# A two-layer decoder trunk on one core: the feed-forward's weight high part streams the tokens' high and low parts as one 512-column matmul

## The chip, the cores and the metric

One core of a Trainium2 chip runs the whole program in one launch. The metric is the device time of that launch in microseconds (us). The median of 3 runs of the kernel before is 1236.72 us, and its runs lie between 1236.55 and 1238.52 us.

## The reference

256 tokens of width 1024 go through two layers. Each layer has two feed-forwards (SwiGLU with 2816 hidden features), a token mixer and a cross-attention, all added to a residual stream in float32. The part that the change touches is the feed-forward, four times in the program:

```python
def swiglu_ffn(x, w_gu, w_down):
    gate, up = jnp.split(x @ w_gu, 2, axis=-1)
    return (jax.nn.silu(gate) * up) @ w_down
...
for layer in range(DEPTH):
    x = x + 0.5 * swiglu_ffn(rms_norm(x, ffn1_norm[layer]), ffn1_w_gu[layer], ffn1_w_down[layer])
    ...
    x = x + 0.5 * swiglu_ffn(rms_norm(x, ffn2_norm[layer]), ffn2_w_gu[layer], ffn2_w_down[layer])
```

`w_gu` is 1024 x 5632 (gate columns first, then up columns) and `w_down` is 2816 x 1024.

## The kernel before

**Two-part products.** A float32 operand is split into two float32r parts, high and low. A dense product is the sum of three matmuls (`mm3`): high times high, high times low and low times high. The normed tokens lie transposed in `xh` and `xl`, as [128 features, 2 token blocks, 8 feature blocks, 128 tokens].

**Weights.** `weights` takes a tile of 128 x 1024 weights from memory into `raw` (4 buffers) by one DMA on SP's queue. ScalarE (ACT) casts it to the high part `wh`, and VectorE (DVE) subtracts to get the low part `wl`. The pool of weight parts has `bufs=10`, for each of the two names. A tile's cast so waits until the matmuls have let go of the tile ten places earlier, and its load waits until the split of the tile four places earlier is done.

**A feed-forward** works through 11 chunks of 256 hidden features. For a chunk `load_chunk` makes four weight tiles: gate columns of feature blocks 0 to 3 and 4 to 7, then the same two of the up columns. There are two ways to do a chunk:

- *Feature-major* (`ws_blocks`): the weight is stationary and all 256 tokens stream. For gate and then up, for each half of 128 hidden features, and for each of the 8 feature blocks k, the three matmuls of `mm3` add 256 columns into half a PSUM bank. All 11 chunks of the first feed-forward and 9 of the 11 in the other three go this way. The first chunk of all has the same matmuls for its gate in another order (`by_pass`, line 296).
- *Token-major*, the first two chunks of the three later feed-forwards: the tokens' part is stationary, and the 256 gate columns and then the 256 up columns of the weight stream. This begins while the second token block is still being normed.

The activation of the gate (ACT), the product with up (DVE) and the split of the result into two parts follow; then `project` multiplies by `w_down` with 512-column matmuls.

**Order.** Dense products call `tick()` with an estimate of their time, and short dependent steps (transposes of a norm, attention pieces) wait in a heap for a number of such ticks. A scheduler then sets each engine's order within the data's dependencies, so loads, casts and subtractions of later tiles stand between the steps of a chunk. The attention parts and `w_down` are not touched by the change, and the order of their instructions is the same in both programs.

Of the kernel before, what the change touches and what calls it, by code (L numbers as in the profile page):

```python
# [12 lines left out]
F32R = mybir.dt.float32r  # L13
BF16 = mybir.dt.bfloat16
AF = mybir.ActivationFunctionType
ALU = mybir.AluOpType
AX = mybir.AxisListType

P = 128
# [8 lines left out]

# How many ns of products to issue between a step and the next one that needs it.
LAG = {  # L30
# [8 lines left out]
def kernel(  # L39
# [45 lines left out]

# [1 line left out]
    clock = [0.0]  # L87
# [34 lines left out]

# [1 line left out]
    xres = [const.tile([P, D], F32, name=f"x{t}") for t in range(2)]  # L124
# [16 lines left out]
    smask = const.tile([P, 3 * P], BF16, name="smask")  # L141
    xh = const.tile([P, 2, NK, P], F32R, name="xh")
    xl = const.tile([P, 2, NK, P], F32R, name="xl")

# [19 lines left out]

# [1 line left out]
    def weights(src):  # L166
        r = raw.tile([P, 1024], F32, name="raw")
        nc.sync.dma_start(r if len(src.shape) == 2 else blocks(r, src.shape[2]), src)
        wh = wsp.tile([P, 1024], F32R, name="wh")
        nc.scalar.copy(wh, r)  # L170
        wl = wsp.tile([P, 1024], F32R, name="wl")
        nc.vector.tensor_tensor(wl, r, f32(wh), op=ALU.subtract)  # L172
        return wh, wl

    def mm3(ps, a, b, start, stop):
        """ps += a.T @ b for two-part operands."""
        nc.tensor.matmul(ps, lhsT=a[0], rhs=b[0], start=start, stop=False)  # L177
        nc.tensor.matmul(ps, lhsT=a[0], rhs=b[1], start=False, stop=False)  # L178
        nc.tensor.matmul(ps, lhsT=a[1], rhs=b[0], start=False, stop=stop)  # L179
# [19 lines left out]
    def transpose4(src):  # L199
        """Four 128-column blocks of src, transposed, in a PSUM bank."""  # L200
        ps = psum() if upcoming.get("starting") else tps()
        for b in range(4):
            nc.tensor.transpose(ps[:, b * P:(b + 1) * P], src[:, b * P:(b + 1) * P], ident)  # L203
        tick(440)
        return ps
# [6 lines left out]
    def norm_T(ss, xt, gain, dst_h, dst_l, tag):  # L212
        """RMSNorm(xt) from its two mean-square halves, transposed, to dst_h, dst_l [P, NK, P]."""
        v = sm.tile([P, 1], F32, name="var")
# [11 lines left out]

# [1 line left out]
    def announce(vec):  # L228
# [28 lines left out]
    def project(view, lhs, evac, nk=NK, tags=(None, None)):  # L257
        """Tokens x 1024 columns: view(k) [P, 1024] of the weight; lhs(t, k) -> parts; evac(t, c, psum)."""
        head = nk - 8
# [29 lines left out]
    def ws_blocks(ps, w, off, per, by_pass=False):  # L289
        """Feature-major: two 128-feature blocks for all tokens into a bank; w tiles of per row blocks."""  # L290
        for b in range(2):
# [12 lines left out]

# [1 line left out]
    def start(load):  # L306
        """The first norm and weights, issued in this order: the loads' own order decides when they come."""
        et = mybir.EngineType
# [17 lines left out]
    def ffn(w_gu, w_down, next_vec, first=False):  # L326
        wv = w_gu.rearrange("(k p) n -> p k n", p=P)
        hts = []

        def load_chunk(c):  # L330
            """[g][k // 4]: gate and up columns of a chunk, four row blocks to a tile."""
            return [[weights(wv[:, 4 * i:4 * i + 4, g * DFF + c * 256:g * DFF + (c + 1) * 256]) for i in range(2)]
                    for g in range(2)]

# [15 lines left out]
        for t in range(2):  # L350
            need(f"x{t}")
            for c in range(0 if first else 2):
                ps = psum()
                for g in range(2):
                    for k in range(NK):
                        mm3(ps[:, g * 256:(g + 1) * 256], xparts(t, k), cols(ws[c][g][k // 4], (k % 4) * 256, 256),
                            k == 0, k == NK - 1)
                        tick(330)
                h = work()
# [12 lines left out]
        for c in range(0 if first else 2, NF // 2):  # L372
            w = ws[0] if first and c == 0 else load_chunk(c)
            if first and c == 2:
                announce(next_vec)
            pg = psum()
            ws_blocks(pg, w[0], 0, 4, by_pass=first and c == 0)
            pu = psum()
            ws_blocks(pu, w[1], 0, 4)
            s = work()  # L380
            nc.scalar.activation(s, pg, AF.Silu)
            h = work()
            nc.vector.tensor_tensor(h, pu, s, op=ALU.mult)
            dh, dl = hslot(c)
            split_to(dh, dl, blocks(h, 256))
# [7 lines left out]

# [1 line left out]
    def gain_col(q, k, parts, factor):  # L395
        """[P, parts]: q*k*factor, per feature of a head, repeated over the partitions."""
        n = q.shape[0] // parts
# [10 lines left out]
    def scale_heads(dst, src, r, n, pair=False):  # L408
        """Heads of n columns, each times its column of r; pair: head i beside head i + half."""
        h = src.shape[1] // n  # L410
# [9 lines left out]
    def attend(groups, scores, values, gap, wait, first=0.0, tag=None, ready=None):  # L420
        """Softmax attention by groups of heads that share a bank of scores.

        scores(g) -> (scores [P, heads, keys], -max [P, heads], denominator columns, where to put exp or None);
        values(g, pT) adds the group's output; ready(g, fn) calls fn once the group's values are issued."""

# [22 lines left out]
    def memory_T(mem_vec, delay):  # L448
        """The memory's norm, transposed in two parts: parts(t, k); issued from delay on."""
        gain = slot()  # L450
# [18 lines left out]
    def head256(dst, gain, tag):  # L469
        """evac: two 256-wide heads normed and transposed into the parts dst[c]; the scale's factor lies in gain."""  # L470
        def evac(t, c, ps):
# [23 lines left out]

# [1 line left out]
    def even_mixer(w_in, q_gain, k_gain, sinks, w_out, next_vec, mem, first=False):  # L497
# [215 lines left out]

# [1 line left out]
    def odd_mixer(w_in, q_gain, k_gain, w_out, next_vec, mem):  # L715
# [104 lines left out]

# [1 line left out]
    class Memory:  # L822
# [11 lines left out]
        def values(self, arrived):  # L834
            """arrived(c) after the values' columns of half c."""
            self.v = [(slot(F32R), slot(F32R)) for _ in range(2)]
# [100 lines left out]
def shape_constants():  # L937
    """Bias and mask tables that depend on positions alone."""
    import ml_dtypes
# [51 lines left out]
```

## Time and profile before

| | |
|---|---|
| median of 3 runs | 1236.72 us (1236.55 to 1238.52) |
| profiled execution, first to last instruction (span) | 1235.6 us, 1.1 us under the median |
| TensorE matmuls (PE) | 7862, busy 1224.9 us, 99% |
| VectorE (DVE), ScalarE (ACT) | busy 713.0 us (58%), 607.7 us (49%) |
| granted TensorE clock | 1.000 over the span |
| moved by DMA | 216.85 MB, mean 176 GB/s |

Matmuls are pipelined: each has a duration of its own that overlaps the next one's, so a busy PE says only that a matmul is always in flight. What a matmul costs in a stream is the distance from its start to the next one's start.

### The profile page before, as it was taken

Reading aid. Unit: us, or ns where it says so; the run is one execution under the profiler, and the core shown is the slowest. Engines: PE = TensorE matmul, PEld = TensorE weight load, DVE = VectorE, ACT = ScalarE, POOL = GpSimd, SP = SyncE. Lnnn points to the kernel's source line nnn. Section 1 sums busy time; section 2 is a strip of 40 time slices with the busy share of each in tenths; the row PEclk is TensorE's granted clock in tenths of the full one; section 3 lists DMA queues with packets and bytes.
Section 4 is the critical chain, followed back from the end, with each engine's and each line's share of the span. In section 5 each row is a group of like instructions: output and inputs, shape, how many; then the busy total and the mean of one; then the engine's idle time right before and its main releaser. Section 6 shows DMA issues by size and latency. Waiting matters only on the chain.

```text
span 1235.6 us, 19425 instructions
## 1 busy us (share of the span) xinstructions
PE 1224.9 (99%) x7862; PEld 1102.4 (89%) x7862; DVE 713.0 (58%) x831; ACT 607.7 (49%) x930; POOL 64.2 (5%) x123
## 2 busy tenths in 40 slices
PE   8999999999999999999999999999999999999998
PEld 6999988887888899998899998888778888999987
DVE  6655545664777675554475555376666776655541
ACT  6544434646565464444354444265644564544430
POOL 1000001200010000000000000033000100000000
PEclk9999999999999999999999999999999999999999
DMA  8866664630454486555386557346633645756550
GB/s 259 260 188 188 205 192 150 247 108 19 136 164 155 152 264 188 178 189 192 98 265 195 186 187 240 120 154 198 217 107 127 195 148 166 230 185 188 175 169 34
DMA packets 134011, 216.85 MB, mean 176 GB/s; under 512 B 7585, under 2 KB 101409, under 8 KB 133922
## 3 DMA queue, kind: packets, MB, share of 16 engines
q1 hardware_dynamic: 133922, 215.62, 54.4%
q8 instruction: 61, 1.00, 0.3%
q14 instruction: 28, 0.23, 0.1%
HBM read 214.54 MB, written 1.05 MB: 174 GB/s over the span
## 4 chain that ended last, share of the span: by engine, by line
PE 94%; DMA 2%; DVE 2%; ACT 1%; issue 1%; POOL 0%; SPq 0%; ACTq 0%; POOLq 0%; DVEq 0%
PE mm L177 29%; PE mm L178 28%; PE mm L179 28%; PE tp L203 3%; PE mm L777 1%; DMA raw<-in_xa_w_o_dram 1%; DVE wl L172 1%; PE mm L798 1%; PE mm L559 1%; PE mm L296 1%; ACT wh L170 1%; DMA x<-in_x_dram 0%; PE mm L580 0%; PE mm L657 0%; ACT junk L209 0%
## 5 line engine op out<-in xcount | busy, mean ns | idle before, releaser
L172 DVE TENSOR_TENSOR wl<-raw,wh 128x1024 fp32r<-128x1024 f32 x386 | 466.9, 1221 | 306.9 <-ACT wh L170 305.6
L170 ACT CAST wh<-raw 128x1024 fp32r<-128x1024 f32 x386 | 401.4, 1051 | 368.0 <-PE mm L178 110.0
L177 PE MATMUL mm<-xh,wh 128*128 128x256 f32 x1264 | 359.8, 285 | 0.0
L178 PE MATMUL mm<-xl,wh 128*128 128x256 f32 x1264 | 357.8, 283 | 0.0
L179 PE MATMUL mm<-xh,wl 128*128 128x256 f32 x1264 | 357.7, 283 | 0.0
L177 PEld LDWEIGHTS mm<-xh,wh 128*128 128x128 f32 x1264 | 242.7, 192 | 1.6 <-issue 1.3
L178 PEld LDWEIGHTS mm<-xl,wh 128*128 128x128 f32 x1264 | 242.8, 192 | 0.0
L179 PEld LDWEIGHTS mm<-xh,wl 128*128 128x128 f32 x1264 | 242.6, 192 | 0.0
L177 PE MATMUL mm<-wh,big 128*128 128x512 f32 x480 | 193.4, 403 | 0.0
L177 PE MATMUL mm<-wh,xh 128*128 128x512 f32 (+1 forms) x528 | 188.7, 357 | 0.0
L179 PE MATMUL mm<-wh,big 128*128 128x512 f32 x480 | 187.3, 390 | 0.0
L178 PE MATMUL mm<-wl,big 128*128 128x512 f32 x480 | 187.2, 390 | 0.0
L178 PE MATMUL mm<-wl,xh 128*128 128x512 f32 (+1 forms) x528 | 184.3, 349 | 0.0
L179 PE MATMUL mm<-wh,xl 128*128 128x512 f32 (+1 forms) x528 | 184.0, 349 | 0.0
L179 PEld LDWEIGHTS mm<-wh,xl 128*128 128x128 f32 x528 | 99.9, 189 | 12.7
L177 PEld LDWEIGHTS mm<-wh,xh 128*128 128x128 f32 x528 | 100.0, 189 | 11.8 <-issue 0.3
L178 PEld LDWEIGHTS mm<-wl,xh 128*128 128x128 f32 x528 | 100.2, 190 | 10.9
L177 PEld LDWEIGHTS mm<-wh,big 128*128 128x128 f32 x480 | 90.3, 188 | 19.0 <-issue 2.0
L179 PEld LDWEIGHTS mm<-wh,big 128*128 128x128 f32 x480 | 90.1, 188 | 19.2
L178 PEld LDWEIGHTS mm<-wl,big 128*128 128x128 f32 x480 | 90.4, 188 | 15.9
L203 PE MATMUL tp<-ident,wk 128*128 128x128 f32 x376 | 56.7, 273 | 1.0 <-DVE wk L417 0.9
L203 PEld LDWEIGHTS tp<-ident,wk 128*128 128x128 f32 x376 | 45.7, 141 | 12.0 <-issue 1.7
(153 smaller groups left out, 841.0 us busy)
## 6 DMA issues: line engine op xcount, KB each, us to landing
raw<-in_ffn_w_gu_dram SPq DMA_DIRECT2D x176, 512.0 KB, 4.6
raw<-in_ffn_w_down_dram SPq DMA_DIRECT2D x88, 512.0 KB, 4.2
raw<-in_xa_w_kv_dram SPq DMA_DIRECT2D x32, 512.0 KB, 5.7
raw<-in_od_w_in_dram SPq DMA_DIRECT2D x24, 512.0 KB, 4.5
raw<-in_ev_w_in_dram SPq DMA_DIRECT2D x18, 512.0 KB, 4.5
raw<-in_xa_w_q_dram SPq DMA_DIRECT2D x16, 512.0 KB, 4.5
raw<-in_xa_w_o_dram SPq DMA_DIRECT2D x16, 512.0 KB, 4.5
raw<-in_ev_w_out_dram SPq DMA_DIRECT2D x8, 512.0 KB, 3.6
```

Source lines behind the costliest of these rows:

```text
L170: nc.scalar.copy(wh, r)
L172: nc.vector.tensor_tensor(wl, r, f32(wh), op=ALU.subtract)
L177: nc.tensor.matmul(ps, lhsT=a[0], rhs=b[0], start=start, stop=False)
L178: nc.tensor.matmul(ps, lhsT=a[0], rhs=b[1], start=False, stop=False)
L179: nc.tensor.matmul(ps, lhsT=a[1], rhs=b[0], start=False, stop=stop)
L203: nc.tensor.transpose(ps[:, b * P:(b + 1) * P], src[:, b * P:(b + 1) * P], ident)
L296: nc.tensor.matmul(ps[:, b * 256:(b + 1) * 256], lhsT=w[k // per][x][:, o:o + P], rhs=xboth(k)[y], start=i == 0 and k == 0, stop=i == 2 an ...
L559: nc.tensor.matmul(sl, lhsT=qaT[hf * 64:(hf + 1) * 64, b, t * P:(t + 1) * P], rhs=kaT[hf * 64:(hf + 1) * 64, 0:keys], start=False, stop=True)
L777: nc.tensor.matmul(ps[:, i * keys:(i + 1) * keys], lhsT=qT[hh][hs, b * 256 + t * P:b * 256 + (t + 1) * P], rhs=kT[hh][hs, b * 256:b * 256 ...
L798: nc.tensor.matmul(po[t, hh][:, (h % 8) * 64:(h % 8 + 1) * 64], lhsT=pt[:, o:o + P], rhs=v[kb][:, h * 64:(h + 1) * 64], start=kb == 0, sto ...
```

## The change

Four edits, all in the feed-forward. `xh` and `xl` become the two halves of one tile `xs`, so that a matmul can read the high and the low tokens of a feature block as 512 columns. A weight tile holds two feature blocks instead of four, each with its 256 gate and 256 up columns side by side, and comes by two DMAs, one for gate and one for up. The feature-major step becomes `ws_wide`: the high weight part streams 512 columns into a whole bank, the low part streams 256 into its first half, and at the end the bank's second half is copied (ACT) and added (DVE). The token-major step streams the 512 gate and up columns in one go. The first chunk of the program stays as it was.

```diff
-    xh = const.tile([P, 2, NK, P], F32R, name="xh")
-    xl = const.tile([P, 2, NK, P], F32R, name="xl")
+    xs = const.tile([P, 2, 2, NK, P], F32R, name="xs")
+    xh, xl = xs[:, 0], xs[:, 1]
...
     def weights(src):
         r = raw.tile([P, 1024], F32, name="raw")
-        nc.sync.dma_start(r if len(src.shape) == 2 else blocks(r, src.shape[2]), src)
+        if len(src.shape) == 4:
+            for g in range(2):
+                nc.sync.dma_start(r.rearrange("p (k g n) -> p k g n", g=2, n=src.shape[3])[:, :, g, :], src[:, :, g, :])
+        else:
+            nc.sync.dma_start(r if len(src.shape) == 2 else blocks(r, src.shape[2]), src)
...
+    def ws_wide(w, g):
+        part, out = work(), work()
+        for b in range(2):
+            ps = psum()
+            for k in range(NK):
+                o = (k % 2) * 512 + g * 256 + b * P
+                wh, wl = cols(w[k // 2], o, P)
+                nc.tensor.matmul(ps, lhsT=wh, rhs=xs[:, :, :, k, :], start=k == 0, stop=False)
+                nc.tensor.matmul(ps[:, 0:256], lhsT=wl, rhs=xh[:, :, k, :], start=False, stop=k == NK - 1)
+                tick(347)
+            bs = slice(b * 256, (b + 1) * 256)
+            nc.scalar.copy(part[:, bs], ps[:, 256:512])
+            nc.vector.tensor_tensor(out[:, bs], ps[:, 0:256], part[:, bs], op=ALU.add)
+        return out
...
         def load_chunk(c):
-            return [[weights(wv[:, 4 * i:4 * i + 4, g * DFF + c * 256:g * DFF + (c + 1) * 256]) for i in range(2)]
-                    for g in range(2)]
+            return [weights(wgu[:, 2 * i:2 * i + 2, :, c * 256:(c + 1) * 256]) for i in range(4)]
...
-                for g in range(2):
-                    for k in range(NK):
-                        mm3(ps[:, g * 256:(g + 1) * 256], xparts(t, k), cols(ws[c][g][k // 4], (k % 4) * 256, 256),
-                            k == 0, k == NK - 1)
-                        tick(330)
+                for k in range(NK):
+                    mm3(ps, xparts(t, k), cols(ws[c][k // 2], (k % 2) * 512, 512), k == 0, k == NK - 1)
+                    tick(650)
...
-            pg = psum()
-            ws_blocks(pg, w[0], 0, 4, by_pass=first and c == 0)
-            pu = psum()
-            ws_blocks(pu, w[1], 0, 4)
+            if first and c == 0:
+                pg = psum()
+                ws_blocks(pg, w[0], 0, 4, by_pass=True)
+                pu = psum()
+                ws_blocks(pu, w[1], 0, 4)
+            else:
+                pg = ws_wide(w, 0)
+                pu = ws_wide(w, 1)
```

On PE, at the start of a feature-major chunk in the first feed-forward, the program before issues three matmuls for each feature block. `mm` is a PSUM bank, and the last row's tile `wl_954` belongs to the same weight tile as `wh_952`.

```order
L179 MATMUL mm_895<-xh_104,wl_844 128x256
L177 MATMUL mm_974<-xh_104,wh_952 128x256 [waits Activation_49]
L178 MATMUL mm_974<-xl_105,wh_952 128x256
L179 MATMUL mm_974<-xh_104,wl_954 128x256 [waits DVE_49]
L177 MATMUL mm_974<-xh_104,wh_952 128x256
```

The changed program issues two there, and goes to the chunk's second weight tile (`wh_1005`) after two feature blocks instead of four:

```order
L319 MATMUL mm_968<-xs_104,wl_905 128x256
L318 MATMUL mm_1025<-xs_104,wh_998 128x512 [waits DVE_49]
L319 MATMUL mm_1025<-xs_104,wl_1000 128x256
L318 MATMUL mm_1025<-xs_104,wh_998 128x512
L319 MATMUL mm_1025<-xs_104,wl_1000 128x256
L318 MATMUL mm_1025<-xs_104,wh_1005 128x512
L319 MATMUL mm_1025<-xs_104,wl_1007 128x256
L318 MATMUL mm_1025<-xs_104,wh_1005 128x512
L319 MATMUL mm_1025<-xs_104,wl_1007 128x256
L318 MATMUL mm_1025<-xs_104,wh_1012 128x512 [waits Activation_49]
```

Each moving pair of 256-column matmuls under one high weight part has become one of 512 columns. The program has 7692 matmuls before and 6220 after, 1472 fewer.

On ACT, one whole chunk of the same stretch before: the gate's activation, the casts of four later weight tiles, which wait for PE to let go of a tile, and the cast of the chunk's result.

```order
L381 ACTIVATE wk_944<-mm_846 128x512 [waits PE_49]
L170 CAST wh_1210<-raw_1208 128x1024 [waits DMAHW1_49,PE_49,Activation_49]
L170 CAST wh_1216<-raw_1214 128x1024 [waits DMAHW2_49,PE_49,Activation_49]
L185 CAST big_818<-wk_946 128x512 [waits DVE_49]
L170 CAST wh_1222<-raw_1220 128x1024 [waits DMAHW3_49,PE_49,Activation_49]
L170 CAST wh_1228<-raw_1226 128x1024 [waits DMAHW4_49,PE_49,Activation_49]
```

And after, from one chunk's first copy (gate, first half) to its last cast:

```order
L322 COPY wk_793<-mm_795 128x256 [waits PE_49,Activation_49]
L189 CAST big_761<-wk_759 128x512 [waits DVE_49]
L322 COPY wk_793<-mm_814 128x256 [waits PE_49]
L322 COPY wk_833<-mm_835 128x256 [waits PE_49]
L404 ACTIVATE wk_873<-wk_794 128x512 [waits DVE_49]
L174 CAST wh_1012<-raw_1009 128x1024 [waits DMAHW2_49,DMAHW1_49,PE_49]
L174 CAST wh_1019<-raw_1016 128x1024 [waits DMAHW4_49,DMAHW3_49,PE_49]
L322 COPY wk_833<-mm_854 128x256 [waits PE_49]
L174 CAST wh_1112<-raw_1109 128x1024 [waits DMAHW6_49,DMAHW5_49]
L174 CAST wh_1119<-raw_1116 128x1024 [waits DMAHW7_49,DMAHW0_49]
```

Four copies are new. The four casts, which stood in two pairs half a chunk apart, now stand together around the chunk's last copy: `wh_1012` and `wh_1019` are the third and fourth tile of the chunk after next, `wh_1112` and `wh_1119` the first and second of the chunk behind that. DVE has the four matching additions beside its four subtractions, and the feed-forward's multiplication now reads two SBUF tiles.

## Rows read from the trace of the kernel before

**Rows 1.** The page's span, its busy time by engine and the granted clock.

```profile
span 1235.6 us, 19425 instructions
...
PE 1224.9 (99%) x7862; PEld 1102.4 (89%) x7862; DVE 713.0 (58%) x831; ACT 607.7 (49%) x930; POOL 64.2 (5%) x123
...
PEclk9999999999999999999999999999999999999999
```

**Rows 2.** The page's chain that ended last, by engine.

```profile
PE 94%; DMA 2%; DVE 2%; ACT 1%; issue 1%; POOL 0%; SPq 0%; ACTq 0%; POOLq 0%; DVEq 0%
```

**Rows 3.** PE's groups by shape, whole program: moving tile, stationary tile, count, mean duration.

```profile
L177 PE MATMUL mm<-xh,wh 128*128 128x256 f32 x1264 | 359.8, 285 | 0.0
...
L177 PE MATMUL mm<-wh,xh 128*128 128x256 f32 x208 | 59.8, 288 | 0.0
```

**Rows 4.** PE's groups in 459.87 to 557.8 us, a feature-major stretch of 97.93 us.

```profile
L179 PE MATMUL mm<-xh,wl 128*128 128x256 f32 x273 | 77.3, 283 | 0.0
L177 PE MATMUL mm<-xh,wh 128*128 128x256 f32 x272 | 77.1, 283 | 0.0
L178 PE MATMUL mm<-xl,wh 128*128 128x256 f32 x272 | 77.0, 283 | 0.0
```

**Rows 5.** PE's groups in 1171.7 to 1231.3 us, the last `w_down`, 59.6 us.

```profile
L177 PE MATMUL mm<-wh,big 128*128 128x512 f32 x88 | 34.2, 389 | 0.0
L178 PE MATMUL mm<-wl,big 128*128 128x512 f32 x88 | 34.2, 389 | 0.0
L179 PE MATMUL mm<-wh,big 128*128 128x512 f32 x87 | 33.8, 389 | 0.0
```

**Rows 6.** PE's timeline where 256-column matmuls give way to 512-column ones.

```profile
557.62 0.28 PE L178 MATMUL mm<-xl,wh 128*128 128x256 f32 x1
557.74 0.28 PE L179 MATMUL mm<-xh,wl 128*128 128x256 f32 x1
557.86 0.40 PE L177 MATMUL mm<-wh,big 128*128 128x512 f32 x1
558.10 0.40 PE L178 MATMUL mm<-wl,big 128*128 128x512 f32 x1
```

**Rows 7.** PE's timeline at four 128-column transposes.

```profile
612.29 0.60 PE L203 MATMUL tp<-ident,wk 128*128 128x128 f32 x4
```

**Rows 8.** DVE's and ACT's groups by shape: count, busy us, mean ns.

```profile
L172 DVE TENSOR_TENSOR wl<-raw,wh 128x1024 fp32r<-128x1024 f32 x386 | 466.9, 1221 | 306.9 <-ACT wh L170 305.6
L383 DVE TENSOR_TENSOR wk<-mm,wk 128x512 f32<-128x512 f32 x38 | 25.9, 683 | 0.0
L361 DVE TENSOR_TENSOR wk<-mm,wk 128x256 f32<-128x256 f32 x12 | 5.0, 418 | 1.8 <-ACT wk L360 1.8
L170 ACT CAST wh<-raw 128x1024 fp32r<-128x1024 f32 x386 | 401.4, 1051 | 368.0 <-PE mm L178 110.0 <-PE mm L179 97.1 <-issue 85.9
L185 ACT CAST big<-wk 128x512 fp32r<-128x512 f32 x38 | 23.6, 621 | 16.8 <-DVE wk L383 16.7
L185 ACT CAST big<-tp 128x256 fp32r<-128x256 f32 x12 | 4.4, 368 | 5.8 <-PE tp L366 5.8
```

**Rows 9.** Stretches: us, busy time (count) by engine, granted clock, DMA share, GB/s.

```profile
429.30:453.80 24.50, 24.50 (x207) 24.46 (x206) 18.79 (x22) 14.96 (x20) 1.11 (x2) 1.00 0.81 261
453.80:557.80 104.00, 104.00 (x869) 104.00 (x868) 54.29 (x57) 49.01 (x57) 0.00 (x0) 1.00 0.62 194
```

**Rows 10.** DMA issues of the gate and up weights, and SP's time to issue four.

```profile
raw<-in_ffn_w_gu_dram SPq DMA_DIRECT2D x176, 512.0 KB, 4.6
...
3.01 2.19 SPq L168 DMA_DIRECT2D raw<-in_ffn_w_gu_dram  x4
```

**Rows 11.** The second feed-forward's start: DVE's and PE's timelines.

```profile
435.05 2.39 DVE L172 TENSOR_TENSOR wl<-raw,wh 128x1024 fp32r<-128x1024 f32 x2
438.39 1.29 DVE L186 TENSOR_TENSOR xl<-tp,xh 128x512 fp32r<-128x512 f32 x2
...
441.23 0.36 PE L177 MATMUL mm<-wh,xh 128*128 128x256 f32 x1
```

More of the change, by code (lines that the diff above doesn't have):

```diff
@@ L327, in ffn @@
         wv = w_gu.rearrange("(k p) n -> p k n", p=P)
+        wgu = w_gu.rearrange("(k p) (g n) -> p k g n", p=P, g=2)
         hts = []
         def load_chunk(c):
-            return [[weights(wv[:, 4 * i:4 * i + 4, g * DFF + c * 256:g * DFF + (c + 1) * 256]) for i in range(2)]
-                    for g in range(2)]
+            return [weights(wgu[:, 2 * i:2 * i + 2, :, c * 256:(c + 1) * 256]) for i in range(4)]
         def hslot(c):
```

## The prediction

> **What bounds the kernel now.** I read the page's busy times first. Of a span of 1235.6 us TensorE has a matmul in flight for 1224.9, at the full granted clock, while DVE is busy for 713.0 and ACT for 607.7 [rows 1]. Busy alone proves little for a pipelined engine, so the chain that ended last comes next: 94% of it is PE, and no other engine has more than 2% [rows 2]. The kernel is bound by the stream of matmuls, and what counts is how many there are and how far apart they start.
>
> That distance comes from a stretch that holds one kind of matmul alone. In 97.93 us of the second feed-forward's feature-major chunks stand 273 + 272 + 272 = 817 matmuls of 256 columns [rows 4]: 97.93 / 817 = 119.9 ns from start to start. The mean of one, 283 ns, is its length in the pipeline and is not used. In the last `w_down` 88 + 88 + 87 = 263 matmuls of 512 columns fill 59.6 us [rows 5]: 226.6 ns each. The timeline at the change from one kind to the other shows the same steps, 0.12 us and then some 0.23 us, and nothing extra for the change [rows 6].
>
> At the granted clock of 1.00, which is 2.4 GHz, 256 columns take 106.7 ns and 512 take 213.3. So 13.2 and 13.3 ns are left over: a cost for each matmul with its new stationary part, however wide it is. Twice the columns double the first part and not the second. No stretch used here has a visible wait: two kinds of matmul, hundreds each, both leave the same rest.
>
> **The change, part by part.**
>
> *Feature-major steps.* Per feature block three matmuls of 256 columns, 3 x 119.9 = 359.7 ns, become one of 512 and one of 256, 226.6 + 119.9 = 346.5 ns: 13.2 ns saved. The number of steps: 37 chunks (10 in the first feed-forward, 9 in each of three others), each with gate and up, two halves and 8 feature blocks, 37 x 32 = 1184. The x1264 rows of the trace are these, 16 of the first chunk and 64 of the even mixer, which don't change [rows 3]. Saved: 1184 x 13.2 = **15.6 us**.
>
> The 512-column form itself, which gathers the tokens from four runs of 128 columns in `xs`, is in no row of before. I take 226.6 ns for it, because the 256-column matmul that streams two runs of 128 tokens and the one that streams 256 adjacent weight columns have the same mean, 285 and 288 ns [rows 3]: gathering has no price there. From above it is bounded by the two matmuls that it replaces, 239.8 ns. From below the pair is bounded by a narrow one that goes as fast as a new stationary part allows: four transposes of 128 columns, each 273 ns long, take 0.60 us together [rows 7], so they start (600 - 273) / 3 = 109 ns apart; then the pair takes 226.6 + 109 = 335.6.
>
> The Trainium skill, "TensorE: Matmul & The Clock Gate", section Back-to-back issue gap, gives N / 2.4 GHz plus about 2.5 ns for a lone warm matmul's gap, so by its figure a matmul saved would be worth 2.5 ns. The trace disagrees: every stationary part here is new, and 13.2 ns are left over. By the page's figure the whole change would save 1472 x 2.5 ns = 3.7 us.
>
> *Token-major steps.* Two token blocks, two chunks and 8 feature blocks in three feed-forwards make 96 steps. In each, six matmuls of 256 columns (6 x 119.9 = 719.4 ns) become three of 512 (679.8): 39.6 ns saved, 96 x 39.6 = **3.8 us**. Here stationary and streamed operands are those of the `project` loops, so the 226.6 ns rest on rows of the same kind.
>
> *Copies and additions.* Each feature-major chunk gains four ACT copies of 128x256 out of PSUM and four DVE additions of the same size. The nearest rows are 368 ns (an ACT cast out of PSUM) and 418 ns (a DVE multiplication of PSUM by SBUF) [rows 8]. A chunk then lasts 32 x 346.5 ns = 11.1 us on PE. ACT has in it four casts at 1051, four copies at 368 and two of about 0.6 us, 6.9 us; DVE four subtractions at 1221, four additions at 418 and two at 683, 7.9 us. Both fit, so I cost them at nothing; what hides them is PE's own stream. Their price uncovered would be (1.5 + 1.7) us x 37 = 118 us. Nothing on PE waits for them soon: a bank is needed again only after five others, 5 x 8 x 346.5 ns = 13.9 us later, and the result of a chunk is read in `w_down`.
>
> *Weight tiles.* A chunk's first block now reads all four tiles within its 2.8 us; before, two tiles served the first half of the chunk. And they are let go only in its last 2.8 us, so the four casts come in one burst. The burst doesn't serve the next chunk: with ten tiles in hand, those let go in one chunk make room for the third and fourth tile of the chunk after next and for two tiles behind these, as the cast order shows. The third one's slot is free 9.0 us into a chunk and the tile is needed 23.6 us into the same count, two chunks and two feature-block pairs on: 14.6 us for a cast and a subtraction of 2.3 us, even behind others. The loads of four tiles, at 194 GB/s in the stretch of before [rows 9], must come 4% faster (11.5 us a chunk become 11.1); 261 GB/s flow a little earlier [rows 9].
>
> *Two DMAs for one.* SP issues four in 2.19 us, 0.55 each, and a tile's load lands after 4.6 us [rows 10]. Eight issues per chunk take 4.4 of 11.1 us on a queue that mostly waits for the splits, so I cost them at nothing; behind them stand only later loads. At worst a load lands half a microsecond later, within the 14.6.
>
> *The start of a later feed-forward* is the tightest place, since the tokens of the second block and the weights both come just then. PE begins that block at 441.23 us; with 16 steps of 39.6 ns saved it would come to it at 440.6. The tokens' low part is done at 438.39 + 1.29 = 439.68 [rows 11], 0.9 us earlier. The second chunk's last tile is the first of the two subtractions that start at 435.05, three microseconds before its use. So nothing new is late, and I take no loss; 1 us at each of three places would be the loss without that cover.
>
> **The sum.** 15.6 + 3.8 = 19.4 us. The profiled span goes from 1235.6 to 1216.2; with the 1.1 us that the median lies above the span, the time goes from 1236.7 to **1217.3 us**, 1.6% faster.
>
> **The rivals.**
>
> *The wide matmul saves nothing.* If streaming four runs costs as much as two matmuls, the first term is gone and only the token-major steps gain: 1236.7 - 3.8 = 1232.9 us. The equal means of rows 3 speak against it.
>
> *The rest isn't the matmul's.* If what is left over beside the streaming belonged to the columns, or came from somewhere else than the number of matmuls, fewer matmuls would bring nothing in either term: 1236.7 us. Against it stands that the rest doesn't grow from 256 to 512 columns. The Trainium skill's 2.5 ns per matmul (page and section above) would be a mild form of this, 1233.0 us.
>
> *PE waits at each chunk's start* (the rival on the other side). If a chunk's tiles were split only as the chunk before lets them go, the last would be ready after one cast and four subtractions, 1.05 + 4 x 1.22 = 5.9 us, counted from the first release 0.7 us into the last block of 2.8, so 6.6 us into it, and used 2.1 us into the next block, at 4.9: it comes 1.7 us late. 37 x 1.7 = 63 us of waiting against 19.4 saved: 1280 us. It decides from 19.4 / 37 = 0.52 us per chunk. For it speaks that casts already wait for PE 110.0 + 97.1 us [rows 8]; against it the ten tiles in hand, and that PE's spacing shows no trace of those waits.
>
> *More than forecast.* A narrow matmul behind a wide one starts the next at the 109 ns of the transposes: 10.9 ns more per step, 12.9 us, 1204.4 us. Against it: the matmuls of 256 columns keep 119.9 ns though their stationary parts could load as fast as the transposes' do.
>
> *The change doesn't do what it says*, say wide matmuls split in two again: the built order shows them whole and 1472 fewer, so only the first rival's time could come of it, and I give it no chance of its own.
>
> **How the numbers follow.** Forecast 0.86, the wide one saves nothing 0.04, the rest isn't the matmul's 0.02, more than forecast 0.04, waits 0.04. The forecast's own range is 1214.5 to 1221.5: a nanosecond either way on each of three distances per step is 3.6 us at most, less or more, and small waits of 1 us at a few places add on the upper side only. For 8 in 10 that range nearly does; as the unknown gathering can cost part of its bound (half of 13.2 ns would be 7.8 us, 1225.1), I reach from 1212 to 1225. Within 0.2% (2.5 us), about what a measurement can tell from no change, would need nearly all of both terms gone. Faster 0.94, same 0.02, slower 0.04.
>
> **What the profile after would show.** A feature-major stretch of nine chunks has 576 matmuls, half of them wide, in 99.8 us instead of 103.6, an average of 173 ns; token-major passes step by 0.68 us per feature block. ACT has 148 new copies near 370 ns, DVE 148 new additions near 420. No idle time of PE before the first matmul of a chunk, and casts still waiting for PE, not PE for casts. I am wrong if wide matmuls start their successor after clearly more than 230 ns, if PE's idle time behind `wh` or `wl` rises by microseconds, or if loads of 256 KB land so late that ACT's casts hold its copies, and with them the banks.

## The result, and the profile after

| | before | after |
|---|---|---|
| median (4 runs each, same chip) | 1237.62 us (1236.55 to 1238.60) | 1219.81 us (1217.32 to 1222.03) |
| span of the profiled execution | 1235.6 us | 1218.6 us (its time 1220.4) |
| matmuls recorded | 7862 | 6390 |

The ratio is 0.9864, with a 95% interval of 0.9850 to 0.9878: 17.8 us faster, where 19.4 were forecast. The forecast of 1217.3 us is 2.5 us under the median, and the median lies in both ranges. What is left to explain is a small shortfall, and most of it turns out to lie in one term.

The page's span, busy times, granted clock and chain after, against [rows 1, 2]:

```profile
span 1218.6 us, 17064 instructions
...
PE 1209.0 (99%) x6390; PEld 1023.5 (84%) x6390; DVE 762.2 (63%) x979; ACT 648.1 (53%) x1078; POOL 63.8 (5%) x123
...
PEclk9999999999999999999999999999999999999999
...
PE 95%; DVE 1%; DMA 1%; ACT 1%; issue 0%; POOL 0%; SPq 0%; ACTq 0%; POOLq 0%; DVEq 0%
```

TensorE is still the bound, at the same clock. There are 148 more ACT and 148 more DVE instructions, and the chain has no more of either engine than before. The groups after (count, busy us, mean ns, idle time before them and what ended it), against [rows 3, 8]:

```profile
L174 ACT CAST wh<-raw 128x1024 fp32r<-128x1024 f32 x386 | 394.0, 1051 | 156.2 <-PE mm L183 80.0
L318 PE MATMUL mm<-xs,wh 128*128 128x512 f32 x1184 | 413.7, 394 | 0.0
L319 PE MATMUL mm<-xs,wl 128*128 128x256 f32 x1184 | 331.8, 280 | 0.0
...
L322 ACT COPY wk<-mm 128x256 f32<-128x256 f32 x148 | 55.3, 374 | 152.0 <-PE mm L319 151.6
L323 DVE TENSOR_TENSOR wk<-mm,wk 128x256 f32<-128x256 f32 x148 | 62.3, 421 | 96.9 <-ACT wk L322 96.9
```

Of the changed feature-major step, L318 is the wide matmul (512 columns) and L319 the narrow one (256). The copies (L322) take 374 ns and the additions (L323) 421; 368 and 418 were taken for them. PE's waits (us in total, times, longest):

```profile
PE mm L333 <- DMA big<-in_ffn_norm_dram: 2.4, 1, 2.4
PE mm L207 <- DVE wk L226: 2.1, 2, 1.1
PE tp L207 <- DVE wk L440: 0.8, 2, 0.5
PE mm L300 <- ACT wh L174: 0.6, 1, 0.6
```

These are norms, an attention step and the first chunk. The view has no row for L318 or L319, so no matmul of a changed feature-major chunk waits for a weight or a bank. So the shortfall must lie in the distances between matmuls. PE's timeline after (start, length), the whole first feed-forward from its second chunk:

```profile
27.40 0.40 PE L318 MATMUL mm<-xs,wh 128*128 128x512 f32 x1
...
59.91 0.40 PE L318 MATMUL mm<-xs,wh 128*128 128x512 f32 x1
60.15 0.28 PE L319 MATMUL mm<-xs,wl 128*128 128x256 f32 x1
60.27 0.40 PE L318 MATMUL mm<-xs,wh 128*128 128x512 f32 x1
60.50 0.28 PE L319 MATMUL mm<-xs,wl 128*128 128x256 f32 x1
60.62 0.40 PE L318 MATMUL mm<-xs,wh 128*128 128x512 f32 x1
60.85 0.28 PE L319 MATMUL mm<-xs,wl 128*128 128x256 f32 x1
60.98 0.40 PE L318 MATMUL mm<-xs,wh 128*128 128x512 f32 x1
...
140.47 0.40 PE L181 MATMUL mm<-wh,big 128*128 128x512 f32 x1
```

From 27.40 to 140.47 stand 10 chunks of 32 steps: 113.07 us / 320 = 353.3 ns a step, not 346.5. Three steps, 59.91 to 60.98, are one period: the wide matmul starts its successor after 236, 232 and 240 ns in turn (0.24, 0.23 and 0.23 in the rows, whose starts are rounded to 0.01 us). Eight chunks of the fourth feed-forward:

```profile
1066.11 0.39 PE L318 MATMUL mm<-xs,wh 128*128 128x512 f32 x1
1066.34 0.28 PE L319 MATMUL mm<-xs,wl 128*128 128x256 f32 x1
1066.45 0.39 PE L318 MATMUL mm<-xs,wh 128*128 128x512 f32 x1
...
1154.86 0.39 PE L181 MATMUL mm<-wh,big 128*128 128x512 f32 x1
```

Here 256 steps take 1154.86 - 1066.11 = 88.75 us, 346.7 ns each, all alike: 230 ns behind a wide matmul and 117 behind a narrow one. The same two instructions in the same order thus run in one of two rhythms, called **tight** (346.7 ns) and **loose** (353.3 ns) from here on. In this execution loose are the first feed-forward and the first 15 steps of the feature-major chunks of each later one, up to two transposes; all else is tight, but for the first two steps behind a transpose. A view that groups by line tells them apart too: a wide matmul is 391 ns long on average where all are tight and 399 where all are loose, and 394 over the program above.

The books of the span begin with the feature-major chunks. PE's timeline before, where those of the first feed-forward begin and end, and where a later one's begin (their end, 557.86, is in [rows 6]):

```profile
27.40 0.28 PE L177 MATMUL mm<-xh,wh 128*128 128x256 f32 x1
...
142.60 0.40 PE L177 MATMUL mm<-wh,big 128*128 128x512 f32 x1
...
453.89 0.36 PE L177 MATMUL mm<-xh,wh 128*128 128x256 f32 x1
```

And where that later one's end after:

```profile
550.99 0.39 PE L181 MATMUL mm<-wh,big 128*128 128x512 f32 x1
```

The first feed-forward's ten chunks take 113.07 us instead of 115.20. The second one's nine, from 450.74, take 100.25 instead of 103.97, and those of the third and fourth the same, 3.7 us less each: 2.1 + 3 x 3.7 = 13.3 us (1184 steps in 413.4 us, before in 426.7). The token-major part of the second feed-forward, from its first matmul to the first feature-major one, takes 427.33 to 450.74, 23.41 us; before it was 429.43 to 453.89, 24.46 us. That is 1.05 us, and 3.2 for the three. PE's first step comes at 12.02 us instead of 12.72, a difference of the program's start of which no step of the prediction speaks. 13.3 + 3.2 + 0.7 = 17.2 us, against 17.0 between the spans.

### The profile page after: what moved, and what is told of

Its sections match the earlier page's. It is cut to its first block, busy times and chain, and to the rows that moved or that the text cites. A ratio compares the mean times of both kernels' runs of the same rounds, so it can differ in the third digit from the quotient of the medians.

```text
span 1218.6 us, 17064 instructions
## 1 busy us (share of the span) xinstructions
PE 1209.0 (99%) x6390; PEld 1023.5 (84%) x6390; DVE 762.2 (63%) x979; ACT 648.1 (53%) x1078; POOL 63.8 (5%) x123
## 3 DMA queue, kind: packets, MB, share of 16 engines
HBM read 214.54 MB, written 1.05 MB: 177 GB/s over the span
## 4 chain that ended last, share of the span: by engine, by line
PE 95%; DVE 1%; DMA 1%; ACT 1%; issue 0%; POOL 0%; SPq 0%; ACTq 0%; POOLq 0%; DVEq 0%
PE mm L318 22%; PE mm L181 18%; PE mm L182 17%; PE mm L183 17%; PE mm L319 12%; PE tp L207 3%; PE mm L800 1%; DMA raw<-in_xa_w_o_dram 1%; PE mm L821 1%; DVE wl L176 1%; PE mm L582 1%; PE mm L300 1%; DMA x<-in_x_dram 0%; PE mm L603 0%; PE mm L680 0%
## 5 line engine op out<-in xcount | busy, mean ns | idle before, releaser
L318 PE MATMUL mm<-xs,wh 128*128 128x512 f32 x1184 | 413.7, 394 | 0.0
L319 PE MATMUL mm<-xs,wl 128*128 128x256 f32 x1184 | 331.8, 280 | 0.0
L318 PEld LDWEIGHTS mm<-xs,wh 128*128 128x128 f32 x1184 | 221.8, 187 | 50.4
L319 PEld LDWEIGHTS mm<-xs,wl 128*128 128x128 f32 x1184 | 223.8, 189 | 0.0
L181 PE MATMUL mm<-wh,xs 128*128 128x512 f32 (+1 forms) x432 | 171.9, 398 | 0.0
L182 PE MATMUL mm<-wl,xs 128*128 128x512 f32 (+1 forms) x432 | 167.6, 388 | 0.0
L183 PE MATMUL mm<-wh,xs 128*128 128x512 f32 (+1 forms) x432 | 167.3, 387 | 0.0
L322 ACT COPY wk<-mm 128x256 f32<-128x256 f32 x148 | 55.3, 374 | 152.0 <-PE mm L319 151.6
L323 DVE TENSOR_TENSOR wk<-mm,wk 128x256 f32<-128x256 f32 x148 | 62.3, 421 | 96.9 <-ACT wk L322 96.9
L183 PEld LDWEIGHTS mm<-wh,xs 128*128 128x128 f32 x432 | 81.2, 188 | 16.5
L181 PEld LDWEIGHTS mm<-wh,xs 128*128 128x128 f32 x432 | 81.3, 188 | 15.2 <-issue 0.3
L182 PEld LDWEIGHTS mm<-wl,xs 128*128 128x128 f32 x432 | 81.4, 188 | 14.3
```

Of the source, the lines that this page charges most:

```text
L318: nc.tensor.matmul(ps, lhsT=wh, rhs=xs[:, :, :, k, :], start=k == 0, stop=False)
L319: nc.tensor.matmul(ps[:, 0:256], lhsT=wl, rhs=xh[:, :, k, :], start=False, stop=k == NK - 1)
L322: nc.scalar.copy(part[:, bs], ps[:, 256:512])
L323: nc.vector.tensor_tensor(out[:, bs], ps[:, 0:256], part[:, bs], op=ALU.add)
```

## The experiments

The kernels of one group share their runs of the kernel before. Two explanations stood for the loose rhythm: TensorE's own state, which a break in the stream sets anew, or something outside PE that comes and goes (copies and additions, loads).

### First group (before: median 1236.90 us)

**The changed kernel unaltered**, for a second profile.

> The changed kernel unaltered, run again to see how its time and its step spacing repeat. In its first profile a feature-major step (one 512-column and one 256-column matmul) came in two patterns: 353.3 ns on average in the first feed-forward and in the first gate half after each token-major part, 347.0 ns in the rest. Theory A (the pattern is set by what last broke the stream, and holds until the next break): the same stretches show the same patterns, 353 ns from 27 to 140 us, 347 ns from 457 us on, and the median is 1218 to 1221 us. Theory B (the slower pattern comes from the load of the first stage: weights just arriving, copies and additions beside them): also 353 ns early. Theory C (chance of each execution): the patterns lie in other stretches, and the time varies by up to some 5 us.

Measured: 1221.17 us, ratio 0.9874 (0.9859 to 0.9889). This time the first feed-forward is loose. The second and third are tight, and the fourth loose, each but for its first 15 steps, which have the other rhythm. The wide matmul's mean length within the second and within the fourth feed-forward:

```profile
L318 PE MATMUL mm<-xs,wh 128*128 128x512 f32 x247 | 85.7, 391 | 0.0
...
L318 PE MATMUL mm<-xs,wh 128*128 128x512 f32 x230 | 81.3, 399 | 0.0
```

The same program therefore doesn't always have its loose stretches in the same places.

**Wide and narrow grouped**: the eight wide matmuls of a half block, then its eight narrow ones.

```diff
-            for k in range(NK):
+            for i in range(2):
+                for k in range(NK):
...
+                    if i == 0:
+                        nc.tensor.matmul(ps, lhsT=wp, rhs=xs[:, :, :, k, :], start=k == 0, stop=False)
+                    else:
+                        nc.tensor.matmul(ps[:, 0:256], lhsT=wp, rhs=xh[:, :, k, :], start=False, stop=k == NK - 1)
...
```

> In each half block the eight 512-column matmuls come first and the eight 256-column ones after them, instead of alternating; same matmuls, copies and additions. Theory A (alternating has a slower pattern of its own, pure streams have none): the steps cost what the pure streams before cost, 226.6 + 119.9 = 346.5 ns, in the first feed-forward too, so 320 + 48 steps gain 6.8 ns, 2.5 us: 1217.3 us. Theory B (load of the first stage): that stretch stays at 353 ns a step and the time at about 1219.8 us. Slower if the low weight parts or banks come late, which neither expects.

Measured: 1221.70 us, ratio 0.9878 (0.9863 to 0.9892); the step is 349.2 ns in every stretch, neither rhythm and not the 346.5 expected. Its PE timeline:

```profile
459.76 1.11 PE L322 MATMUL mm<-xs,wl 128*128 128x256 f32 x8
460.71 2.00 PE L320 MATMUL mm<-xs,wh 128*128 128x512 f32 x8
462.55 1.12 PE L322 MATMUL mm<-xs,wl 128*128 128x256 f32 x8
```

Eight wide ones take 462.55 - 460.71 = 1.84 us, 230 ns each, where 226.6 were expected; the narrow ones take 0.95 / 8 = 119 ns. In the trace's records the first five wide ones behind narrow ones take 233, 236, 229, 232 and 231 ns and only then 227, and the first two narrow ones 113 and 119. A return from narrow to wide costs about 20 ns in all, net of what the narrow ones win.

**A nudge**: two transposes that nobody reads, between gate and up of the second chunk of the first feed-forward.

```diff
                 pg = ws_wide(w, 0)
+                if first and c == 1:
+                    nudge = tps()
+                    for b in range(2):
+                        nc.tensor.transpose(nudge[:, b * P:(b + 1) * P], h[:, b * P:(b + 1) * P], ident)
                 pu = ws_wide(w, 1)
```

> Two 128-column transposes, whose result nobody reads, are put between the gate and the up half of the second chunk of the first feed-forward, as two transposes stood where the pattern changed in the later feed-forwards. They cost about 0.3 us. Theory A (the pattern is set by what last broke the stream): from there on, about 33 us, the steps go at 347.0 instead of 353.3 ns, about 300 steps: 1.9 us less, 1.6 net, 1218.2 us. Theory B (load of the first stage): the steps stay at 353 ns up to 140 us, and the time is 1220.1 us.

Measured: 1220.91 us, ratio 0.9872 (0.9854 to 0.9890). Its PE timeline around the nudge, and where the feed-forward's chunks end:

```profile
31.91 0.39 PE L405 MATMUL tp<-ident,wk 128*128 128x128 f32 x2
32.05 0.48 PE L318 MATMUL mm<-xs,wh 128*128 128x512 f32 x1
...
137.42 0.28 PE L319 MATMUL mm<-xs,wl 128*128 128x256 f32 x1
137.53 0.39 PE L181 MATMUL mm<-wh,big 128*128 128x512 f32 x1
```

The 304 steps behind the nudge take 137.53 - 32.05 = 105.48 us, 347.0 ns each. The feed-forward that was loose in all three profiles of the changed kernel is tight for its whole length behind two small matmuls. Nothing came of it in the total, since the second feed-forward, behind its first 15 steps, is loose in this profile.

**Without the sum**: copies and additions are left out, and with them the high weight part times low tokens of gate and up, in all chunks but the first; the matmuls are all there.

```diff
...
-            nc.scalar.copy(part[:, bs], ps[:, 256:512])
-            nc.vector.tensor_tensor(out[:, bs], ps[:, 0:256], part[:, bs], op=ALU.add)
+            out.append(ps)
...
+                    nc.scalar.activation(s[:, bs], pg[b][:, 0:256], AF.Silu)
+                    nc.vector.tensor_tensor(h[:, bs], pu[b][:, 0:256], s[:, bs], op=ALU.mult)
...
```

> The copies and additions at the end of each feature-major block are left out: the activation and the product read the first half of each bank, so the part of high weight times low tokens is left out of gate and up. 148 ACT copies of 0.37 us and 148 DVE additions of 0.42 us go, two activations and two multiplications of 256 columns take the place of one of 512 each. Theory (they lie beside PE's stream and cost nothing): the time is that of the changed kernel within 1 us, 1219 to 1221 us, and the step spacing is the same. Rival (they hold banks or weight tiles, or disturb PE): some of their 55 + 62 us shows, over 2 us less, and the early steps go at 347 ns.

Measured: 1222.19 us, ratio 0.9880 (0.9865 to 0.9895), mean step 350.6 ns. The wide matmul in its first feed-forward:

```profile
L318 PE MATMUL mm<-xs,wh 128*128 128x512 f32 x318 | 112.4, 399 | 0.0
```

The copies and additions cost no time that can be measured, and the loose rhythm is there without them.

### Second group (before: median 1237.25 us)

**The layout alone**: `xs`, the mixed weight tiles and the two DMAs for one, but only matmuls of 256 columns.

```diff
...
-                nc.tensor.matmul(ps, lhsT=wh, rhs=xs[:, :, :, k, :], start=k == 0, stop=False)
-                nc.tensor.matmul(ps[:, 0:256], lhsT=wl, rhs=xh[:, :, k, :], start=False, stop=k == NK - 1)
+                mm3(ps[:, b * 256:(b + 1) * 256], cols(w[k // 2], o, P), xboth(k), k == 0, k == NK - 1)
...
-                    mm3(ps, xparts(t, k), cols(ws[c][k // 2], (k % 2) * 512, 512), k == 0, k == NK - 1)
+                        mm3(ps[:, g * 256:(g + 1) * 256], xparts(t, k),
+                            cols(ws[c][k // 2], (k % 2) * 512 + g * 256, 256), k == 0, k == NK - 1)
...
```

> The layout alone: tokens in one tile, weight tiles of two feature blocks with gate and up side by side, two DMAs each, all four tiles of a chunk needed by its first block; but the matmuls are those of before, three of 256 columns per step, 7692 in all, and no copies or additions. Theory A (the gain is the number of matmuls times 13.3 ns): no change from before, 1236 to 1238 us. Rival (the layout or the two loads cost something, which hid 2 us of the gain): 1239 us or more. Rival (better loads gave part of the gain): 1234 us or less.

Measured: 1237.00 us, ratio 0.9995 (0.9986 to 1.0003): nothing. Tiles needed four at a time, released in one burst, and twice the DMA issues, are hidden.

**Layout and the wide token-major step** (only the first of the two edits above).

> The layout and the token-major matmuls of 512 columns; the feature-major steps stay three matmuls of 256. 288 matmuls fewer than before. Theory A: 96 steps x 39.6 ns = 3.8 us less than before, 1233 us. If the gain isn't per matmul: 1237 us.

Measured: 1234.56 us, ratio 0.9977 (0.9967 to 0.9988): 2.7 us less.

**Layout and the wide feature-major step** (only the second).

> The layout and the feature-major steps of one 512-column and one 256-column matmul; the token-major matmuls stay 256 wide. 1184 matmuls fewer than before. By the forecast's step of 346.5 ns: 15.6 us less, 1221.3 us. By the two patterns seen, between 347.0 ns (all steps fast: 15.2 us less, 1221.7 us) and 353.3 ns (all steps slow: 7.7 us less, 1229.2 us): I expect 1223 to 1226 us, with one stretch at least in each pattern.

Measured: 1229.24 us, ratio 0.9930 (0.9918 to 0.9942), 8.0 us less, under what was expected. The wide group of its profile:

```profile
L318 PE MATMUL mm<-xs,wh 128*128 128x512 f32 x1184 | 418.9, 399 | 0.0
```

With 399 ns the mean is that of the loose rhythm. Its 1184 steps take 418.6 us, 353.5 each: it is loose everywhere but in the first 15 steps of each later feed-forward, although the feature-major instructions are those of the changed kernel. That gains 426.7 - 418.6 = 8.1 us, and the time shows it. So the two parts measured alone, 2.7 + 8.0, don't add up to the whole change: which rhythm the stretches fall into differs between the programs.

**A whole chunk grouped**: 32 wide matmuls into four banks, then 32 narrow ones.

```diff
+        halves = [(g, b) for g in range(2) for b in range(2)]
+        ps = [psum() for _ in halves]
+        for i in range(2):
+            for n, (g, b) in enumerate(halves):
+                for k in range(NK):
...
```

> All 32 matmuls of 512 columns of a chunk first, in four banks, then its 32 of 256. Grouping by eights gave 349.2 ns a step in every stretch: the first wide matmuls behind narrow ones took 233, 236, 229, 232, 231 ns before they settled at 226.7, and the first narrow one 113, a net cost of 20 ns for each return to wide ones. Theory (that cost is paid per return): one return per 32 steps, 346.7 + 20 / 32 = 347.3 ns in every stretch, 1184 x 1.9 ns = 2.2 us under the grouping by eights, 1219.4 us beside its 1221.7, and no slow pattern anywhere. Rival (the order brings waits: four banks are held at once, low weight parts to the end of the chunk): idle time of PE at the chunk's start and 1222 us or more.

Measured: 1241.48 us, ratio 1.0034 (1.0017 to 1.0051), slower than before. Without waits its step is 347.3 ns, as expected; but PE waits now. Its waits:

```profile
PE mm L181 <- DVE wk L329: 9.7, 4, 2.7
PE mm L318 <- DVE wk L329: 3.5, 7, 1.5
```

Its PE timeline at one such wait, at the start of `w_down`:

```profile
142.80 0.39 PE L183 MATMUL mm<-wh,big 128*128 128x512 f32 x1
145.63 0.50 PE L181 MATMUL mm<-wh,big 128*128 128x512 f32 x1 [2.45 <-DVE wk L329]
```

And ACT's timeline there, with what ended its idle time:

```profile
143.80 1.04 ACT L174 CAST wh<-raw 128x1024 fp32r<-128x1024 f32 x1 [1.24 <-DMA raw<-in_ffn_w_down_dram]
144.76 0.64 ACT L328 COPY wk<-mm 128x256 f32<-128x256 f32 x2
```

L329 is the addition that frees a bank. It needs the copy, and the copy stands on ACT behind a cast that waits for its load until 143.80. In the changed kernel one bank is taken at a time and the same queue costs nothing; with four of the six in hand until a chunk's end, PE feels it. The wait costs clock as well. In the stretch from 146.0 to 149.4 us, just behind the 2.45 us in which PE stood still (the columns are those of [rows 9], the granted clock third from the end):

```profile
146.00:149.40 3.40, 3.40 (x10) 2.63 (x9) 3.40 (x6) 1.42 (x4) 0.00 (x0) 0.50 0.33 72
```

The granted clock is 0.50 there, the lower of TensorE's two levels (1.2 GHz), and so it is behind the same wait in the second feed-forward, 2.69 us long. Behind the two others, of 2.27 and 2.28 us, it stays at 1.00.

### Third group (before: median 1236.04 us)

**The changed kernel unaltered**, a third time.

> The changed kernel unaltered, beside the two orders below on the same chip. 1219 to 1222 us; which stretches go at 347.0 and which at 353.3 ns a step may differ from the two profiles so far.

Measured: 1221.32 us, ratio 0.9882 (0.9867 to 0.9896). Loose are the first and the third feed-forward, tight the second and the fourth, each later one but for its first 15 steps.

**Half a chunk grouped**: 16 wide into two banks, then 16 narrow.

```diff
+        ps = [psum(), psum()]
+        for i in range(2):
+            for b in range(2):
+                for k in range(NK):
...
```

> Gate, then up: the 16 wide matmuls of both half blocks first, in two banks, then the 16 narrow ones. Theory (20 ns for each return from narrow to wide, and no slow pattern): 346.7 + 20 / 16 = 347.9 ns a step in every stretch, 1184 x 347.9 = 411.9 us for all steps, where the changed kernel's two profiles have 413.4 and 415.2: 1.5 to 3.3 us under it, about 1218 us, and no more spread than the kernel before. Two banks at a time leave four for the copies, so no wait of PE for a bank as in the grouping by a whole chunk. Rival (waits for banks as there): 0.5 us and more per chunk, over 1225 us.

Measured: 1221.23 us, ratio 0.9875 (0.9859 to 0.9892). Its PE timeline:

```profile
43.72 3.82 PE L318 MATMUL mm<-xs,wh 128*128 128x512 f32 x16
47.37 2.08 PE L320 MATMUL mm<-xs,wl 128*128 128x256 f32 x16
49.28 2.91 PE L318 MATMUL mm<-xs,wh 128*128 128x512 f32 x12
```

One return in 16 steps instead of 8: 3.65 / 16 = 228 ns for a wide matmul, and 347.9 ns a step over the stretches, as worked out from 20 ns a return. All steps take 412.4 us, 1 us less than in the first profile of the change, which the times don't resolve.

**By twos**: two wide, two narrow.

```diff
-            for k in range(NK):
+            for k in range(0, NK, 2):
+                for i in range(2):
+                    for j in (k, k + 1):
...
```

> Within a half block two wide matmuls and then two narrow ones, four times. Theory (a return to wide ones costs some 13 to 20 ns before the spacing settles): with 233 and 236 for the wide ones and 113 and 119 for the narrow ones 350.5 ns a step, 1184 x 3.5 = 4.1 us over the fast pattern, 1220 to 1221 us, in every stretch alike. If by twos there is a fast pattern too, 347 ns: 1217 us.

Measured: 1219.27 us, ratio 0.9863 (0.9848 to 0.9878), a step of 348.3 ns in every stretch, where 350.5 were expected, from the first two distances of each kind in the order by eights: (233 + 236 + 113 + 119) / 2. Its PE timeline, ten steps:

```profile
62.44 0.62 PE L321 MATMUL mm<-xs,wh 128*128 128x512 f32 x2
...
65.92 0.40 PE L321 MATMUL mm<-xs,wh 128*128 128x512 f32 x1
```

Distances carried from one order to another missed again. Against the changed kernel beside it (1221.32) the intervals overlap, so no order tried here is shown to beat the change.

## Why the prediction was right, and where its size was off

*The bound and the spacing.* Right. Fewer starts at the same clock made the time shorter by 17.8 us, and by 15.7 and 14.7 in the two later measurements, of the 19.4 forecast. Layout, loads and additions gave nothing and cost nothing by themselves, so the gain is the matmuls'. In the tight rhythm the step is 346.7 ns against the forecast 346.5. That the total came so near is in part luck: the two terms measured 13.3 + 3.2 = 16.5 us, and 0.7 us of the difference between the spans came from the program's start. The range's own working, 3.6 us either way, would begin at 1213.7 and not at 1214.5; nothing hangs on that.

*The feature-major term*, 15.6 us forecast, measured 13.3. This is the term that was mis-sized. It took 226.6 + 119.9 ns from streams of one width and added them. It read "nothing extra for the change" off two wide matmuls behind narrow ones [rows 6], at a step of 0.01 us, too coarse to see 5 or 10 ns. Three rows further down the same timeline something extra does show:

```profile
558.79 0.39 PE L178 MATMUL mm<-wl,big 128*128 128x512 f32 x1
```

That is the fifth wide matmul, 0.93 us behind the first at 557.86: 232 ns each for the first four, where 226.6 was taken. What an alternation one by one costs was in no row, and bounds were put on the gathering instead. Gathering four runs costs nothing that shows: by eights, gathered wide matmuls settle at 227 ns too. The loose rhythm costs 353.3 - 346.5 = 6.8 ns a step, and 365 loose steps (320 + 3 x 15) make 2.5 us, as much as the 2.3 that are missing. Two smaller differences nearly cancel: the first steps behind transposes, some 0.5 us, and 0.8 us by which the steps before took longer than 359.7 ns each (the 817 matmuls of [rows 4] count one that began before the window; from start to start it is 120.0 ns).

*The token-major term*, 3.8 us forecast, measured 3.2, and 2.7 alone (interval 1.5 to 4.1). A like effect is behind it: transposes that waited in the heap stand in the token-major stream, and the wide matmuls behind them are late for a while. PE's timeline after, behind two transposes:

```profile
445.33 0.40 PE L182 MATMUL mm<-wl,xs 128*128 128x512 f32 x1
...
447.65 0.39 PE L183 MATMUL mm<-wh,xs 128*128 128x512 f32 x1
...
450.37 0.39 PE L183 MATMUL mm<-wh,xs 128*128 128x512 f32 x1
450.60 0.38 PE L385 MATMUL tp<-ident,wk 128*128 128x128 f32 x2
450.74 0.48 PE L318 MATMUL mm<-xs,wh 128*128 128x512 f32 x1
```

Ten matmuls from 445.33 to 447.65 start 232 ns apart, the twelve from there to 450.37 only 227. Before, the 256-column matmuls behind the same transposes stepped by 116 to 122 ns from the second one on, no loss at all. Some 45 to 50 ns behind each of three breaks, and a little in the first matmul behind each, are most of the 0.2 us by which each feed-forward misses its 1.27.

*Copies, additions, weight tiles, two DMAs*, costed at nothing: right, by the runs without the sum and of the layout alone. *The start of a later feed-forward*, also at nothing: right, no wait of PE there that before hadn't.

*The rivals.* The wide matmul saves nothing, and the rest isn't the matmul's: both fell, since the steps alone gained 13.3 us. Here a matmul saved is worth 360.0 - 346.7 = 13.3 ns in the tight rhythm, and 6.7 in the loose. By the Trainium skill ("TensorE: Matmul & The Clock Gate", Back-to-back issue gap) a lone warm matmul costs about 2.5 ns beside its columns, and an estimate from that makes one saved worth 2.5 ns; the runs disagree. More than forecast fell too, though in a smaller measure it is there: behind a wide matmul a narrow one starts its successor after 117 ns in the tight rhythm, not 119.9, and the wide one behind it gives those 3 ns back. PE waits at each chunk's start: fell for the weights. The grouped chunk shows what such a wait looks like once the cover, free banks in its case, is gone. Fewer weight tiles in hand, which would test the rival in its own place, were not tried.

*The profile after, as forecast*: a later feed-forward's nine chunks take 450.74 to 550.99, 100.25 us against 99.8; copies and additions near their numbers; no new idle time of PE. The mark set for being wrong, a wide matmul that starts its successor clearly more than 230 ns later, was reached in the loose rhythm (236 on average) without turning the sign.

*Open.* Why a stretch is loose or tight. Shown is that both occur with the same instructions, that copies and additions aren't the cause (the memory traffic wasn't varied by itself), and that a rhythm, once there, lasts to the next break. What a break does is more regular than the runs were planned to see. Six profiles have the alternating order: three of the changed kernel, the nudge, the run without the sum and the wide feature-major step alone. In all 18 later feed-forwards of these the two transposes behind the first 15 steps turn the one rhythm into the other, 11 times from loose to tight and 7 times from tight to loose; the nudge is a nineteenth time. This speaks for something that TensorE's own stream carries on, rather than for loads that come and go, but what it is isn't shown. Nor is it explained which rhythm the chunks of a feed-forward start in: the first feed-forward starts loose in all six, the later ones either way. A cause inside TensorE's weight loading was not tested; the recorded loads, but for about a dozen, are 187 to 190 ns long in both rhythms, so their length doesn't tell them apart.

## What to carry to other kernels

Where every matmul brings a new stationary part, the matmuls count, not their columns alone: put two streams under one stationary part when both fit in one bank (512 columns here), and check that the extra addition falls on engines with time to spare. Take the distance from start to start from a stretch with the very order that the new kernel will have; distances of pure streams, added up, missed 0 to 7 ns a step here. Before an order that holds more banks at once, look at what stands ahead of the instruction that frees them.

## What the runs showed of the hardware that was not expected

- An alternation of 512- and 256-column matmuls runs at 346.7 or at 353.3 ns a pair, in stretches of 5 to 113 us, at a granted clock of 1.00 in both; which it is differs between executions of one program.
- Wide matmuls behind narrow ones or transposes are late for five to ten matmuls, 232 ns instead of 227; narrow ones behind the same transposes lose nothing from the second one on.
- Two 128-column transposes in the alternating stream turned the one rhythm into the other in 19 places of 19, in either direction.
- The order of the same matmuls is worth up to 2% of a step: 346.7 to 353.3 ns singly, 348.3 by twos, 349.2 by eights, 347.9 by sixteens.
